# Squared deviation from the row mean: eight tiles of one row per partition in place of four tiles of two rows

## The chip, the cores and the metric

One core of a Trainium2 chip. The metric is the device time of one execution in microseconds (us), median of several. The kernel before takes 84.68 us (three runs, 84.6 to 84.7). All runs quoted are of the fast state (granted clock 1.000 in each profile), and correct.

## The reference

```python
batch, dim = 1024, 4096                      # x is float32, axis = -1
mean = np.mean(x, axis=axis, keepdims=True)
return ((x - mean) ** 2).astype(np.float32)
```

16.78 MB are read and 16.78 MB written. Everything fits into SBUF at once, so each tile has its own buffer.

## The kernel before

```python
Q = 2
ntiles = B // (P * Q)                                   # 4 tiles
x_t = x.rearrange("(n p q) d -> n p (q d)", p=P, q=Q)   # 32 KiB contiguous per partition
out_t = out.rearrange("(n p q) d -> n p (q d)", p=P, q=Q)
# ... pools with one buffer per tile
for i in range(ntiles):
    x_tile = pool.tile([P, Q * D], mybir.dt.float32)
    nc.sync.dma_start(out=x_tile, in_=x_t[i])           # all loads, on SP's queue
    x_tiles.append(x_tile)
for i in range(ntiles):
    # ... views and small tiles
    nc.vector.reduce_sum(out=neg_sum, in_=x_tile, axis=mybir.AxisListType.X, negate=True)
    nc.vector.tensor_scalar_mul(out=neg_mean, in0=neg_sum, scalar1=inv_d)
    for q in range(Q):
        nc.scalar.activation(out=x_tile[:, q, :], in_=x_tile[:, q, :],
                             func=mybir.ActivationFunctionType.Square,
                             bias=neg_mean[:, q:q + 1], scale=1.0)
    nc.scalar.dma_start(out=out_t[i], in_=x_tiles[i])   # store, on ScalarE's queue
```

Of the kernel before, what the change touches and what calls it, by code (L numbers as in the profile page):

```python
# [2 lines left out]

os.environ.setdefault("NEURON_RT_ULTRASERVER_MODE", "4")

# [4 lines left out]


@with_exitstack
def kernel(
    ctx: ExitStack,
    tc: tile.TileContext,
    x: bass.AP,
    axis: bass.AP,
    out: bass.AP,
):  # L20
    nc = tc.nc

    B, D = x.shape
    P = nc.NUM_PARTITIONS
    Q = 2
    assert B % (P * Q) == 0
    ntiles = B // (P * Q)

    inv_d = 1.0 / float(D)

    x_t = x.rearrange("(n p q) d -> n p (q d)", p=P, q=Q)
    out_t = out.rearrange("(n p q) d -> n p (q d)", p=P, q=Q)

    pool = ctx.enter_context(tc.tile_pool(name="io", bufs=ntiles))
    stats = ctx.enter_context(tc.tile_pool(name="stats", bufs=ntiles))

    x_tiles = []
    for i in range(ntiles):
        x_tile = pool.tile([P, Q * D], mybir.dt.float32)
        nc.sync.dma_start(out=x_tile, in_=x_t[i])  # L40
        x_tiles.append(x_tile)

    for i in range(ntiles):
        x_tile = x_tiles[i].rearrange("p (q d) -> p q d", q=Q)
        neg_sum = stats.tile([P, Q], mybir.dt.float32)
        neg_mean = stats.tile([P, Q], mybir.dt.float32)
        nc.vector.reduce_sum(  # L47
            out=neg_sum,
            in_=x_tile,
            axis=mybir.AxisListType.X,  # L50
            negate=True,
        )
        nc.vector.tensor_scalar_mul(out=neg_mean, in0=neg_sum, scalar1=inv_d)  # L53

        for q in range(Q):
            nc.scalar.activation(  # L56
                out=x_tile[:, q, :],
                in_=x_tile[:, q, :],
                func=mybir.ActivationFunctionType.Square,
                bias=neg_mean[:, q:q + 1],  # L60
                scale=1.0,
            )
        nc.scalar.dma_start(out=out_t[i], in_=x_tiles[i])


# [1 line left out]
_INS = ['x', 'axis']  # L67
_OUTS = [((1024, 4096), 'float32')]
#: Inputs that are plain numbers.
_NUMBERS = {'axis': -1}  # L70


# [26 lines left out]
```

## Time and profile before

| | before |
|---|---|
| time, span | 84.68 us, 82.9 us |
| VectorE, ScalarE busy | 43%, 37% |
| load queue + store queue, share of 16 DMA engines | 48.6% + 47.0% |
| first DMA packet to end of last one | 1.75 to 81.72 us |

Read it from the bottom: the transfers fill the DMA engines from 2 us to the end, and the compute engines wait for them. The lines of the page, the windows and the timeline stand in the prediction below.

The trace has a record of every DMA packet, with start, duration and queue, but without the number of the DMA engine. Since each of the 16 engines takes one packet after another, the records can be strung into 16 chains: each packet goes to the engine whose last packet ended closest to its start. In the kernel before this gives 16 chains of 64 packets each. Neighbouring chains can be confused by a few nanoseconds (in other runs some come out one packet long or short); pauses that all but one engine make cannot. At a hole, "the slowest engine" means the chain that runs dry last.

### The profile page before, as it was taken

The numbers are of one execution on the slowest core, as the hardware profiler recorded it, in microseconds if no ns is written. First come the engines' busy times: TensorE is split into PE (matmuls) and PEld (weight loads), VectorE is DVE, ScalarE is ACT, GpSimd is POOL, SyncE is SP. The second block draws the span as 40 slices with busy tenths as digits, with TensorE's granted clock in tenths as the row PEclk, the third lists the DMA queues.
The fourth block names the chain that finished last, engine by engine and source line by source line (L and its number), as shares of the span: only waits on it lengthen the run. The fifth ranks groups of instructions, "written<-read, shape, count | busy, mean of one in ns | idle before, by whom it ended". The sixth has DMA issues, their size and how long they took to land.

```text
span 82.9 us, 75 instructions
## 1 busy us (share of the span) xinstructions
DVE 35.4 (43%) x8; ACT 30.5 (37%) x9; POOL 0.2 (0%) x4
## 2 busy tenths in 40 slices
DVE  0000007999599995999900000799950000000000
ACT  0000006000399917998099950000049990000000
POOL 0000000000000000000000000000000000000000
DMA  7779997997999899997997999899796996995990
GB/s 190 300 332 443 506 427 332 506 490 316 459 506 411 348 506 285 443 474 316 490 490 332 443 490 427 348 506 474 332 443 285 506 490 269 506 506 253 506 506 0
DMA packets 1153, 33.55 MB, mean 405 GB/s; under 512 B 129, under 2 KB 129, under 8 KB 129
## 3 DMA queue, kind: packets, MB, share of 16 engines
q1 hardware_dynamic: 576, 16.78, 48.6%
q10 hardware_dynamic: 576, 16.78, 47.0%
q14 instruction: 1, 0.00, 0.0%
HBM read 16.78 MB, written 16.78 MB: 405 GB/s over the span
## 4 chain that ended last, share of the span: by engine, by line
DMA 37%; DVE 21%; another core or an unknown queue 13%; ACT 5%; issue 4%; SPq 1%
DMA x_tile<-in_x_dram 37%; DVE neg_sum L47 21%; ACT x_tile L56 5%; SPq L40 1%; DVE neg_mean L53 0%
## 5 line engine op out<-in xcount | busy, mean ns | idle before, releaser
L47 DVE TENSOR_REDUCE neg_sum<-x_tile 128x2 f32<-128x8192 f32 x4 | 34.7, 8686 | 25.6 <-DMA x_tile<-in_x_dram 25.6
L56 ACT ACTIVATE x_tile<-x_tile,neg_mean 128x4096 f32<-128x4096 f32 x8 | 29.2, 3700 | 24.9 <-DVE neg_mean L53 24.9
L56 ACT ACT_TABLE_LOAD x1 | 1.3, 1283 | 13.1 <-DMA x_tile<-in_x_dram 13.1
L53 DVE TENSOR_SCALAR neg_mean<-neg_sum 128x2 f32<-128x2 f32 x4 | 0.7, 170 | 0.1
L80 POOL MEMSET const-bfloat16-1.0<- 128x1 bf16 x1 | 0.1, 102 | 0.0
L80 POOL MEMSET const-uint8-127<- 128x1 uint8 x1 | 0.1, 102 | 0.0
L80 POOL MEMSET const-float32-1.0<- 128x1 f32 x1 | 0.1, 99 | 0.0
L80 POOL MEMSET const-float32-0.0<- 128x1 f32 x1 | 0.1, 98 | 0.2 <-issue 0.2
## 6 DMA issues: line engine op xcount, KB each, us to landing
x_tile<-in_x_dram SPq DMA_DIRECT2D x4, 4096.0 KB, 26.2
out_dram<-x_tile ACTq DMA_DIRECT2D x4, 4096.0 KB, 17.4
```

The source lines that it names most:

```text
L40: nc.sync.dma_start(out=x_tile, in_=x_t[i])
L47: nc.vector.reduce_sum(out=neg_sum, in_=x_tile, axis=mybir.AxisListType.X, negate=True,)
L53: nc.vector.tensor_scalar_mul(out=neg_mean, in0=neg_sum, scalar1=inv_d)
L56: nc.scalar.activation(out=x_tile[:, q, :], in_=x_tile[:, q, :], func=mybir.ActivationFunctionType.Square, bias=neg_mean[:, q:q + 1], scal ...
L80: nc = _bacc.Bacc("TRN2", target_bir_lowering=False, num_devices=1)
```

## The change

Its intent: finer tiles, so that the first reduction and the first store begin earlier and loads, arithmetic and stores overlap more. The loads stay on SP's queue and the stores on ScalarE's, as they were.

```diff
-    Q = 2
-    ntiles = B // (P * Q)
+    ntiles = B // P
-    x_t = x.rearrange("(n p q) d -> n p (q d)", p=P, q=Q)
-    out_t = out.rearrange("(n p q) d -> n p (q d)", p=P, q=Q)
+    x_t = x.rearrange("(n p) d -> n p d", p=P)
+    out_t = out.rearrange("(n p) d -> n p d", p=P)
@@ second loop, cut
-        for q in range(Q):
-            nc.scalar.activation(out=x_tile[:, q, :], in_=x_tile[:, q, :], ...
+        nc.scalar.activation(out=tiles[i], in_=tiles[i], ...
```

More of the change, by code (lines that the diff above doesn't have):

```diff
@@ L10 @@
 from concourse._compat import with_exitstack
+F32 = mybir.dt.float32
 @with_exitstack
@@ L24 @@
     P = nc.NUM_PARTITIONS
-    Q = 2
-    assert B % (P * Q) == 0
-    ntiles = B // (P * Q)
+    assert B % P == 0
+    ntiles = B // P
     inv_d = 1.0 / float(D)
-    x_t = x.rearrange("(n p q) d -> n p (q d)", p=P, q=Q)
-    out_t = out.rearrange("(n p q) d -> n p (q d)", p=P, q=Q)
-    pool = ctx.enter_context(tc.tile_pool(name="io", bufs=ntiles))
-    stats = ctx.enter_context(tc.tile_pool(name="stats", bufs=ntiles))
-    x_tiles = []
+    x_t = x.rearrange("(n p) d -> n p d", p=P)
+    out_t = out.rearrange("(n p) d -> n p d", p=P)
+    io = ctx.enter_context(tc.tile_pool(name="io", bufs=ntiles))
+    stats = ctx.enter_context(tc.tile_pool(name="stats", bufs=2 * ntiles))
+    tiles = []
     for i in range(ntiles):
-        x_tile = pool.tile([P, Q * D], mybir.dt.float32)
+        x_tile = io.tile([P, D], F32)
         nc.sync.dma_start(out=x_tile, in_=x_t[i])
-        x_tiles.append(x_tile)
+        tiles.append(x_tile)
     for i in range(ntiles):
-        x_tile = x_tiles[i].rearrange("p (q d) -> p q d", q=Q)
-        neg_sum = stats.tile([P, Q], mybir.dt.float32)
-        neg_mean = stats.tile([P, Q], mybir.dt.float32)
+        neg_sum = stats.tile([P, 1], F32)
+        neg_mean = stats.tile([P, 1], F32)
         nc.vector.reduce_sum(
-            out=neg_sum,
-            in_=x_tile,
-            axis=mybir.AxisListType.X,
-            negate=True,
+            out=neg_sum, in_=tiles[i], axis=mybir.AxisListType.X, negate=True
         )
         nc.vector.tensor_scalar_mul(out=neg_mean, in0=neg_sum, scalar1=inv_d)
-        for q in range(Q):
-            nc.scalar.activation(
-                out=x_tile[:, q, :],
-                in_=x_tile[:, q, :],
-                func=mybir.ActivationFunctionType.Square,
-                bias=neg_mean[:, q:q + 1],
-                scale=1.0,
-            )
-        nc.scalar.dma_start(out=out_t[i], in_=x_tiles[i])
+        nc.scalar.activation(
+            out=tiles[i],
+            in_=tiles[i],
+            func=mybir.ActivationFunctionType.Square,
+            bias=neg_mean,
+            scale=1.0,
+        )
+        nc.scalar.dma_start(out=out_t[i], in_=tiles[i])
 _INS = ['x', 'axis']
```

## The prediction

> **What bounds the kernel now.** I read four views in this order: the page (busy shares, DMA queues), the table of windows, the timeline, and the time from issue to landing of the two transfers. The page first:
>
> ```profile
> span 82.9 us, 75 instructions
> DVE 35.4 (43%) x8; ACT 30.5 (37%) x9; POOL 0.2 (0%) x4
> q1 hardware_dynamic: 576, 16.78, 48.6%
> q10 hardware_dynamic: 576, 16.78, 47.0%
> HBM read 16.78 MB, written 16.78 MB: 405 GB/s over the span
> ```
>
> No compute engine is half busy, while the two DMA queues (q1 the loads, q10 the stores) together take 48.6 + 47.0 = 95.6% of the 16 DMA engines' span. 576 packets per queue are four transfers of 128 rows (512 packets of 32 KiB) and 64 small completion writes. So the kernel is bound by bytes moved, and the question is only in which stages the DMA engines are not full. The windows answer it (the last two columns are DMA share and GB/s):
>
> ```profile
> 2.20:31.00 28.80, 17.10 (x3) 8.59 (x3) 0.00 (x0) 1.00 0.98 422
> 33.40:51.60 18.20, 7.92 (x2) 12.89 (x4) 0.00 (x0) 1.00 1.00 430
> 61.20:62.05 0.85, 0.00 (x0) 0.85 (x1) 0.00 (x0) 1.00 0.10 39
> 62.05:81.40 19.35, 0.00 (x0) 6.45 (x2) 0.00 (x0) 1.00 1.01 432
> 1.75:81.70 79.95, 35.43 (x8) 30.51 (x9) 0.00 (x0) 1.00 0.99 419
> ```
>
> Loads alone run at 422 GB/s, loads and stores mixed at 430, stores alone at 432: reading and writing together cost nothing. There is one hole, 61.20 to 62.05 us. The timeline shows who made it:
>
> ```profile
> 13.04 8.69 DVE L47 TENSOR_REDUCE neg_sum<-x_tile 128x2 f32<-128x8192 f32 x1 [13.04 <-DMA x_tile<-in_x_dram]
> ...
> 29.30 0.38 ACTq L63 DMA_DIRECT2D out_dram<-x_tile  x1
> ...
> 41.40 0.34 ACTq L63 DMA_DIRECT2D out_dram<-x_tile  x1
> 45.00 3.69 ACT L56 ACTIVATE x_tile<-x_tile,neg_mean 128x4096 f32<-128x4096 f32 x1
> 52.27 8.69 DVE L47 TENSOR_REDUCE neg_sum<-x_tile 128x2 f32<-128x8192 f32 x1 [10.92 <-DMA x_tile<-in_x_dram]
> 60.99 0.17 DVE L53 TENSOR_SCALAR neg_mean<-neg_sum 128x2 f32<-128x2 f32 x1
> 61.20 3.71 ACT L56 ACTIVATE x_tile<-x_tile,neg_mean 128x4096 f32<-128x4096 f32 x1 [12.50 <-DVE neg_mean L53]
> 61.20 0.34 ACTq L63 DMA_DIRECT2D out_dram<-x_tile  x1
> ```
>
> Tile 2 was squared at 45.00 + 3.69 = 48.7 us, but its store was issued at 61.20, beside the first activation of tile 3: in ScalarE's program that store stands behind an activation that has to wait for the last load and its 8.69 us reduction. By 61.2 the store queue had run dry.
>
> The trace's packet records give the rest of the budget. One 32 KiB packet takes 1.213 us on its engine, each engine has 64 of them: 64 x 1.213 = 77.6. The first packet starts at 1.75. The first packet of each engine is slow (0.70 us over the rest, averaged over the 16 engines), and when the first store joins the loads, the loads lose another 0.67. With 0.1 of small change and the hole of 0.85: 1.75 + 0.70 + 77.6 + 0.67 + 0.1 + 0.85 = 81.7, which is where the packets end. The last landing is 0.4 later, the end of the program 0.8 after that (82.9), and the time is 84.68, 1.8 over the span.
>
> **What the Trainium skill says.** (1) "DMA: Bandwidth & Descriptors", section Where 436 GB/s comes from: a fabric ceiling of 435.2 GB/s for the 16 ports. The trace agrees: 16 x 32,768 B / 1.213 us = 432 GB/s, so the steady stages have less than 1% to give. (2) Same page, Issuing engines are not separate DMA queues: issues from different engines end on the same 16 DMA engines and interleave. The trace agrees, and "loads on SP's queue, stores on ScalarE's" is moreover already so in the kernel before. (3) Same page, Queues, rings and completion order: each DMA engine goes round-robin over its queues by packet. The trace agrees: the last load, with 9.7 us of packets per engine, began at 31.5 and landed only at 52.2, as it should at half the rate. (4) "VectorE: DVE Perf Modes", the tier table: tensor_reduce has the 1x rate alone, at 0.96 GHz; 8192 elements would take 8.53 us, the trace has 8.69. So halving the row count halves the instruction.
>
> **The change, part by part.** Bytes, buffers in all, engines and queues stay. What changes is grain.
>
> Packets: 128 of 16 KiB per engine instead of 64 of 32 KiB. In the records an 8 KiB packet[...] takes 0.307 us at best and a 32 KiB one 1.211, so the slope is 0.904 us per 24,576 B and the fixed part 0.307 - 0.301 = some 6 ns. A 16 KiB packet is then 0.608 us (an estimate), and 128 x 0.608 = 77.9: **+0.3 us**, all of it on the path.
>
> VectorE: 8 reductions of 8.69 / 2 = 4.35 (say 4.4) and 8 scalings of 0.17, beside the transfers. ScalarE: the same 8 activations of 3.70. SP: 8 issues of some 0.45 us instead of 4, done by 5 us, while the first tile alone feeds the engines until some 7; nothing.
>
> First tile: lands after 8 packets of 0.608 instead of 1.213, so at 13.0 - 4.8 = 8.2. Reduction to 12.8, activation to 16.5, store issued then instead of at 29.3. In the kernel before it took 4.1 us from that issue (29.30) to the first store packet (33.41), behind packets already under way; I take 2.5 to 4.1 now, so stores start at 19.0 to 20.6. This gains **nothing** by itself: the engines are full with loads at that time, so stores only take turns with loads earlier.
>
> The end: I walk it with stores from 19.0. Loaded by then: (19.0 - 2.9) / 4.87 = 3.3 tiles (4.87 us is a tile alone, 9.73 at half rate). The other 4.7 loads take 4.7 x 9.73 = 45.7, so the last load is in at 64.7; 4.7 tiles are stored by then, and 3.3 remain, 16.1 us, to 80.8. Is the store queue ever dry? The compiled order on ScalarE is Act0, St0, Act1, Act2, St1, St2, Act3, Act4, St3, St4, Act5, Act6, St5, St6, Act7, St7, so the odd stores are still held behind the next activation. St3 goes with the start of Act4: tile 4 lands at 35.5, plus 4.5 is 40.0; needed at 48.2. St5 goes with Act6: 55.0 + 4.5 = 59.5; needed at 67.4 at the latest, some 66 at the earliest. St7: 64.7 + 0.5 (landing) + 4.5 + 3.7 = 73.4, plus 0.85 from issue to first packet = 74.3; St6 ends at 80.8 - 4.87 = 75.9. Margin 1.6 us, and more if the stores start later. So the hole goes: **-0.85 us**.
>
> Sum: 81.7 + 0.3 - 0.85 = 81.1 for the last packet, span 82.3, time 84.1. I add 0.2 for unevenness between the 16 engines, which twice as many landings may expose: **84.3 us**, 0.4% faster.
>
> **The rivals.** (a) A new hole at the end: if one engine lags by over 1.6 us at the last load, St7 comes late. For it: one load packet took 2.2 us when the stores joined, and the last load's 16 landings spread over 2.2 us. Against: the others spread over about 1 us or less. It would cost 0.5 to 1.5: 84.8 to 85.8. (b) The longer mixed stage (19 to 65 instead of 33 to 52) or the smaller packets run slower. For it: the 0.67 us lost when the stores joined. Against: 430 GB/s in the mixed window. If each 16 KiB packet lost 20 ns more, 128 x 0.02 = 2.6 us: 86.9, slower by over 2%. (c) A real gain from the earlier start, as the change intends: overlap of load, compute and store. Against: the DMA engines are full from 2 us on. Even with the hole, the joining loss and the slow first packets all gone, it is 84.68 - 0.85 - 0.67 - 0.70 = 82.5; 2% faster is 83.0, so nearly all three would have to go, and two of them are untouched.
>
> **Range and chances.** The low end, 83.6, is the sum with half of the joining loss gone; the high end, 85.4, is rival (a) in its middle. Faster by over 2% 0.02, slower 0.05 (rival b, or a hole of 2 us), within 2% 0.93.
>
> **What would show it.** Right: two queues of 1152 packets at 47 to 49% each; first reduction near 8.2 us, first store issue near 16.5; last load landing near 65; DMA at 430 GB/s through 20 to 80 with no window of 1 us or more empty; reductions near 4.4 us. Wrong: a mixed stage under 420 GB/s (rival b), or DMA idle before the last store (rival a). If reductions or activations end the chain with DMA idle beside them, my picture of a transfer-bound kernel fails.

## The result, and the profile after

| | before | after | foretold |
|---|---|---|---|
| time, first comparison | 84.65 us (4 runs) | 84.69 us (4 runs, 84.46 to 84.75) | 84.3 |
| ratio, first comparison | | 1.0002, 95% interval 0.9983 to 1.0020 | 0.9955 |
| ratio, second comparison | | 0.9983, 0.9962 to 1.0004 | 0.9955 |
| last DMA packet ends | 81.72 us | 81.81 us | 81.1 |

A ratio is the mean time of one kernel's fast runs over that of the other's in the same rounds, so it is not quite the ratio of the medians. All outputs are right. The time did not move: the range and "within 2%" held, the small gain (0.4%) did not come.

The page after, the same lines:

```profile
span 83.0 us, 96 instructions
DVE 36.6 (44%) x16; ACT 30.9 (37%) x9; POOL 0.2 (0%) x4
q1 hardware_dynamic: 1152, 16.78, 49.0%
q10 hardware_dynamic: 1152, 16.78, 47.2%
HBM read 16.78 MB, written 16.78 MB: 404 GB/s over the span
```

Twice the packets for the same bytes at the same share. The timeline after (start, duration, what):

```profile
8.58 4.42 DVE L46 TENSOR_REDUCE neg_sum<-x_tile 128x1 f32<-128x4096 f32 x1 [8.58 <-DMA x_tile<-in_x_dram]
...
16.96 0.38 ACTq L57 DMA_DIRECT2D out_dram<-x_tile  x1
...
60.10 4.07 ACTq L57 DMA_DIRECT2D out_dram<-x_tile  x2
65.17 4.42 DVE L46 TENSOR_REDUCE neg_sum<-x_tile 128x1 f32<-128x4096 f32 x1 [5.11 <-DMA x_tile<-in_x_dram]
...
73.55 0.34 ACTq L57 DMA_DIRECT2D out_dram<-x_tile  x1
```

The first store goes at 16.96 instead of 29.30, as intended; the last reduction begins later than before (65.17, not 52.27), because the loads now share the engines with stores for longer. The windows after (last two columns: DMA share, GB/s):

```profile
17.00:22.00 5.00, 4.68 (x3) 3.71 (x1) 0.00 (x0) 1.00 0.98 364
22.00:64.00 42.00, 19.21 (x10) 18.54 (x5) 0.00 (x0) 1.00 1.00 430
61.20:62.05 0.85, 0.00 (x0) 0.85 (x1) 0.00 (x0) 1.00 0.99 424
```

The hole of the kernel before (0.85 us at share 0.10) is filled: 0.99. And there is no other one. Yet the last packet ends no earlier. So what was the hole worth?

The packet chains answer. This is how each engine of the kernel **before** went through the hole (worked out from the packet records, ns; one number per engine):

```
pause at 62 us, 16 engines: 0 170 402 497 574 584 616 623 657 705 741 756 797 824 866 898   mean 607
```

The engine with pause 0 is the one that ends the kernel: it was still at its store packets until 62.36 us, while the others had run dry from 61.27 on and had begun again between 62.05 and 62.17. Then the ends of the last packet:

| us | first engine | mean | last engine |
|---|---|---|---|
| before | 81.53 | 81.59 | 81.72 |
| after | 81.12 | 81.34 | 81.81 |
| after, second profile | 81.00 | 81.22 | 81.63 |

The change did make the mean engine earlier, by 0.25 to 0.37 us. The last one, which the kernel waits for, stayed within 0.1 us of where it was.

### The profile page after: what moved, and what is told of

Same layout as the page of the kernel before. It is cut to its first block, busy times and chain, and to the rows that moved or that the text cites. A ratio compares the mean times of both kernels' runs of the same rounds, so it can differ in the third digit from the quotient of the medians.

```text
span 83.0 us, 96 instructions
## 1 busy us (share of the span) xinstructions
DVE 36.6 (44%) x16; ACT 30.9 (37%) x9; POOL 0.2 (0%) x4
## 3 DMA queue, kind: packets, MB, share of 16 engines
q1 hardware_dynamic: 1152, 16.78, 49.0%
q10 hardware_dynamic: 1152, 16.78, 47.2%
## 4 chain that ended last, share of the span: by engine, by line
DMA 77%; DVE 6%; ACT 4%; SPq 1%; issue 0%
DMA x_tile<-in_x_dram 77%; DVE neg_sum L46 5%; ACT x_tile L50 4%; SPq L40 1%; DVE neg_mean L49 0%
## 5 line engine op out<-in xcount | busy, mean ns | idle before, releaser
L46 DVE TENSOR_REDUCE neg_sum<-x_tile 128x1 f32<-128x4096 f32 x8 | 35.4, 4420 | 32.9 <-DMA x_tile<-in_x_dram 32.9
L50 ACT ACTIVATE x_tile<-x_tile,neg_mean 128x4096 f32<-128x4096 f32 x8 | 29.7, 3708 | 33.9 <-DVE neg_mean L49 33.9
L49 DVE TENSOR_SCALAR neg_mean<-neg_sum 128x1 f32<-128x1 f32 x8 | 1.2, 154 | 0.3
```

Of the source, the lines that this page charges most:

```text
L46: nc.vector.reduce_sum(out=neg_sum, in_=tiles[i], axis=mybir.AxisListType.X, negate=True)
L50: nc.scalar.activation(out=tiles[i], in_=tiles[i], func=mybir.ActivationFunctionType.Square, bias=neg_mean, scale=1.0,)
```

## The experiments

Two theories. **A**: the end is set by the slowest of the 16 DMA engines; in the hole only the faster ones waited for it, so filling it gives them time that nobody needs. **B**: the hole cost the kernel 0.6 (mean pause) to 0.85 us as predicted, and something in the finer grain costs as much. Each ratio is to the kernel before on the same chip, in five rounds.

### The hole alone: queues exchanged, two-row tiles

```diff
-        nc.sync.dma_start(out=x_tile, in_=x_t[i])
+        nc.scalar.dma_start(out=x_tile, in_=x_t[i])
-        nc.scalar.dma_start(out=out_t[i], in_=x_tiles[i])
+        nc.sync.dma_start(out=out_t[i], in_=x_tiles[i])
```

> The kernel before with the queues exchanged: loads issued by ScalarE, stores by SP, so that no store stands behind an activation and the third store goes at about 49 us, not 61.2. The hole at 61.2 closes. Theory A (the end is set by the slowest of the 16 DMA engines, which never paused in that hole; only the 15 faster ones did): 84.5 to 84.75 us, no gain. Theory B (the hole cost all engines 0.6 to 0.85 us, and the finer packets of the change ate the gain): 83.8 to 84.1 us.

Measured: 84.58 us (six runs, 84.03 to 84.85), ratio 0.9975 (0.9949 to 1.0000). The third store goes at 48.71, and the window of the hole is full (the share counts packets at their start, so it can pass 1 in a short window):

```profile
48.71 0.33 SPq L63 DMA_DIRECT2D out_dram<-x_tile  x1
```

```profile
61.20:62.05 0.85, 0.04 (x1) 0.77 (x1) 0.00 (x0) 1.00 1.35 578
62.05:81.40 19.35, 0.00 (x0) 6.53 (x2) 0.00 (x0) 1.00 0.95 410
```

No engine pauses by more than 0.05 us any more. The first engine ends at 80.66, the mean at 80.99, the last at 81.91: the mean engine gained the whole 0.60 us, the last gained nothing (81.72 before). (The profiled run of this kernel was the slowest of its six, 84.85 us.) The second line shows it from the other side: 410 GB/s at the end, where the kernel before had 432, because engines that are done idle beside the late ones. That is A. It isn't all of it: the ratio says 0.2 us with an interval from 0 to 0.4, and one of six runs came at 84.03, as B would have it. A guess, not shown: without a hole the time depends on how unequal the engines happen to be in that execution. These six runs scatter over 0.82 us, the kernel before over 0.37 in the same rounds; but the changed kernel, which has no hole either, scatters over 0.29 us and, in the second comparison, 0.12.

### The control: queues exchanged, one-row tiles

The same edit in the changed kernel.

> The changed kernel with the queues exchanged in the same way: no store is held behind an activation. There was no hole in the changed kernel, so both theories say the same: 84.5 to 84.8 us. A time under 84.2 would say that the holding back of the odd stores cost something that neither theory has.

Measured: 84.64 us, ratio 0.9988 (0.9972 to 1.0005). As foretold: the exchange of queues and the end of the holding back of every second store, taken together, change nothing.

### The grain alone: two-row tiles, 16 KiB packets

```diff
-    x_t = x.rearrange("(n p q) d -> n p (q d)", p=P, q=Q)
-    out_t = out.rearrange("(n p q) d -> n p (q d)", p=P, q=Q)
+    x_t = x.rearrange("(n q p) d -> n p q d", p=P, q=Q)
+    out_t = out.rearrange("(n q p) d -> n p q d", p=P, q=Q)
```

> The kernel before with its two-row tiles, engines and order, but the two rows of a partition lie 128 rows apart, so every packet is 16 KiB. Only the grain of the transfers changes. Theory A (some 6 ns more per packet, 64 packets more on each DMA engine, +0.4 us, less what a shorter first and joining packet gives back): 84.7 to 85.1 us. Theory B (the grain costs as much as the hole was worth, 0.6 to 0.85): 85.25 to 85.5 us.

Measured: 84.64 us, ratio 0.9989 (0.9975 to 1.0003): below both ranges, so A missed here too. The packets are not free: on one engine they follow each other every 607 ns instead of two in 1210, and in the changed kernel every 607.8, so 128 x 0.6078 - 64 x 1.2097 = 0.38 us per engine. But this kernel still has the hole, and the records show that it swallowed the cost: the mean pause is 0.25 us instead of 0.61, and the last engine ends at 81.67. Whatever an engine loses ahead of the hole, it loses out of its own waiting time. For the same reason the time of this run alone can't exclude a grain cost of B's size: a cost up to the mean pause, 0.61 us, could have been swallowed too. The spacing does, with 0.38 us instead of 0.6 to 0.85, and so does the next run. (In this trace the engine that ends last, at 81.67, did pause, by 0.41 us; the one that didn't pause ends at 81.58. All 16 ends lie within 0.15 us.)

### The grain, four times finer

SBUF tiles of the changed kernel padded every 4 KiB (`x_wide = io.tile([P, 4, D // 4 + 8], F32)`, used through `x_wide[:, :, : D // 4]`), so that each packet is 4 KiB; the reduction runs over both inner axes.

> The changed kernel with SBUF tiles padded every 4 KiB, so that packets are 4 KiB: 512 per DMA engine instead of 128. Theory A, 5.8 ns fixed per packet: 384 more make +2.2 us, 86.7 to 87.2 us. Theory B, 64 more packets cost 0.6 to 0.85 us, so 9 to 13 ns each: 384 more make +3.6 to +5.1 us, 88.3 to 89.8 us.

Measured: 86.47 us, ratio 1.0201 (1.0184 to 1.0217). Against the exchanged one-row kernel (84.64), +1.8 us; A's range began 0.2 us higher, B's 1.8. On one engine packets follow each other every 155.5 ns: 512 x 0.1555 - 128 x 0.6078 = +1.8 us. From 4 and 16 KiB the fixed part is 4.7 ns per packet, from 16 and 32 KiB 5.8. There is no hole here to hide it. So the prediction's term for the grain (+0.3) was right, with some luck: its 6 ns came from 8 KiB packets of another queue, which the profile calls instruction packets.

### A hole on purpose, short and long

A copy in place between the last activation and the last store of the changed kernel, over 2400 or 4096 columns:

```diff
+        if i == ntiles - 1:
+            nc.scalar.activation(out=tiles[i][:, :2400], in_=tiles[i][:, :2400],
+                                 func=mybir.ActivationFunctionType.Copy)
         nc.scalar.dma_start(out=out_t[i], in_=tiles[i])
```

> The changed kernel with a copy of 2400 columns in place between the last activation and the last store: the last store is issued at some 75.9 instead of 73.55, its first packets at some 76.8. In the trace of the changed kernel the 16 DMA engines end the store before between 76.3 and 76.95, so most engines pause, the slowest does not. Theory A (the slowest engine sets the end): no cost, within 0.15 us of the changed kernel. Theory B (mean idle of the engines counts): +0.3 us.

> The same with 4096 columns: the last store is issued at some 77.35, its first packets at some 78.2, 1.25 us after the slowest engine has run dry and 1.7 after the mean one. Theory A: +1.1 to +1.4 us over the changed kernel. Theory B: +1.6 to +1.8 us.

And beside them, as their base:

> The changed kernel unchanged, for a closer interval and as the base of the two delays of the same call. All theories: 84.5 to 84.8 us, within 0.3% of the kernel before.

Measured: base 84.56 us (0.9983); short 84.65 (0.9992, 0.9967 to 1.0017); long 85.92 (1.0140, 1.0115 to 1.0165). The timeline of the long one:

```profile
73.53 3.62 ACT L58 ACTIVATE x_tile<-x_tile 128x4096 f32<-128x4096 f32 x1
77.18 0.34 ACTq L63 DMA_DIRECT2D out_dram<-x_tile  x1
```

and its window at the hole, in which no packet starts at all:

```profile
76.60:78.00 1.40, 0.00 (x0) 0.55 (x1) 0.00 (x0) 1.00 0.00 0
```

In the long one the engines paused 1.11 us (the slowest) to 1.98, on average 1.71; the time rose by 85.92 - 84.56 = 1.36. That lies in A's range and below B's. In the short one 13 of 16 engines paused, up to 0.49 us and 0.20 on average, the last to end did not; the time rose by 0.09. This agrees with A, but the intervals are as wide as the 0.2 to 0.3 us that B asks for, so the short one alone would decide nothing.

### Where the engines grow unequal

In the records of before, most of it comes at two places: the first packet of each engine (up to 1.2 us over the rest) and the moment when the first store's packets join the loads (0.67 us per engine on average before, 0.66 after, 0.4 to 1.5 on single engines). The slowest engine of before started at 2.27, lost 0.55 in its first packet and some 1.4 at the joining; with 64 x 1.210 = 77.4 that makes 81.7, its end, with no pause in it.

Is the joining loss one of the store queue's first use?

> The changed kernel with the load of the second tile alone on ScalarE's queue, which the stores use later. Two questions: does a start from two queues fill the engines sooner (a gain of up to 0.3 us), and is the loss when the first store joins (0.66 us per engine) one of a queue's first use (then it vanishes, and with it part of the spread between the engines: 84.0 to 84.3 us) or of two queues beginning to share an engine (then it stays: 84.4 to 84.8)? I expect the second.

Measured: 84.48 us, ratio 0.9970 (0.9949 to 0.9992), within the range of the answer that I expected. Load packets are long by 0.83 us per engine around 28 to 30 us, when the stores join. First use is not it. The edit did one more thing: tile 0 now shares the engines with tile 1, so the first reduction begins at 12.90 us and the first store is issued at 26.13, not near 17. As for the first question, the engines' first packets start at 1.87 us on average, against 1.90 in the unchanged kernel of the same call: no gain to speak of. The 0.1 us against that kernel's time (84.56) is within the noise.

### When the stores begin

```diff
+        if i == 0:
+            zero = stats.tile([P, 1], F32)
+            nc.gpsimd.tensor_scalar_mul(out=zero, in0=tiles[6][:, 0:1], scalar1=0.0)
+        if i < 6:   # the store cannot go before load 6 has landed
+            nc.gpsimd.tensor_tensor(out=tiles[i][:, 0:1], in0=tiles[i][:, 0:1], in1=zero,
+                                    op=mybir.AluOpType.add)
         nc.scalar.dma_start(out=out_t[i], in_=tiles[i])
```

> The changed kernel with all stores held until the load of tile 6 has landed, some 37.5 us instead of 17.0 (GpSimd adds 0 times a column of tile 6 to a column of tiles 0 to 5; the result stays right). The DMA engines still have the last load to do when the stores begin, so they never run dry. Theory A (bytes on always full engines set the time; when stores begin is worth nothing): 84.4 to 85.0 us. The intent of the change (storing earlier shortens the run): 20 us less overlap should show as several us.

Measured: 84.36 us (84.15 to 84.38), ratio **0.9953** (0.9940 to 0.9966). The first store is issued at 38.44 us:

```profile
38.44 5.16 ACTq L66 DMA_DIRECT2D out_dram<-x_tile  x6
```

The time is 0.04 us under A's range. Stores that begin 21 us later make it not slower but slightly faster than the kernel before, and probably than the changed one, which was compared with it only in other calls (1.0002 and 0.9983). The intent of the change, storing earlier, is worth nothing here. The hold also let SP issue all eight loads by 4.85 us, where the changed kernel issued the last at 18.34; that isn't the gain, since the control with exchanged queues issued its eight by 4.95 us and ran at 0.9988. The five microseconds in which stores take over, to set beside 17 to 22 us of the changed kernel above (0.98 and 364 GB/s):

```profile
38.50:43.50 5.00, 4.01 (x3) 2.83 (x1) 0.67 (x5) 1.00 0.99 419
43.50:80.00 36.50, 4.51 (x2) 7.42 (x2) 0.00 (x0) 1.00 1.01 432
```

The same share, but 419 GB/s: **busy is not moving**. In the changed kernel the load packets stretched while the stores joined and the share stayed near 1; only the rate shows it. Here the last load's packets are long by 0.07 us per engine instead of 0.66. The first store's packets began at 41.65, just as the loads ran out. All engines end earlier: first 80.55, mean 80.84, last 81.31.

Held until the last load, on the other hand, all 16 engines run dry together:

> The same, held until the last load has landed (some 42.5 us). Now all 16 engines run dry, the slowest too, from its last load packet (some 42.2) over the landing, two small GpSimd instructions and the issue to the first store packet, some 1.5 to 2 us; loads and stores never share an engine, so the joining loss (0.66) and its part of the spread go. Theory A: 85.2 to 86.2 us.

Measured: 86.62 us, ratio 1.0227 (1.0213 to 1.0241), above my range.

```profile
41.60:44.10 2.50, 2.19 (x3) 1.68 (x1) 1.11 (x7) 1.00 0.00 0
```

The pauses were 1.93 us on the engine with the shortest and 2.72 on the longest; I had counted 1.5 to 2. The rest of the miss: after such a common restart packets followed each other every 613.7 ns instead of 607.8 (64 x 5.9 = 0.4 us). The kernel before shows the same after its hole, 1217 ns against 1209.7 ahead of it. Why is open.

Held until load 4 only:

> As the hold until the load of tile 6 (which ran at 0.9953 of the kernel before, with no joining loss in its packets), but held only until the load of tile 4 has landed, some 27.5 us; the first stores are issued at some 28.3 and their packets should join at some 31.5, with about two loads still queued. If the loss of 0.5 to 0.8 us per engine comes whenever stores join a load queue that still has work, it is back: loads' packets long by that much around 31, 84.5 to 84.8 us (0.998 to 1.001 of the kernel before). If it came only of an early or a first use, it stays away: 0.994 to 0.997, 84.2 to 84.45 us.

Measured: 84.51 us, ratio 0.9971 (0.9951 to 0.9991): the time is at the foot of the first answer's range, the ratio between the two. The packets show the loss back in part: 0.42 us per engine around 31 to 33 us, when two loads were still queued. So the loss has to do with stores joining a queue that still has loads, and is smaller when fewer are left; what in the engine makes it is open.

A last attempt, three two-row tiles and then two of one row, with the same hold:

> An attempt to beat both: three tiles of two rows (32 KiB packets), then two of one row; stores held until the fourth load has landed (some 37.5 us), so that they follow the loads without a gap and hardly share the engines with them. Against the hold until load 6: 80 packets per engine instead of 128, 48 x 5.8 ns = 0.28 us less at best; the grain experiment showed about nothing of it in the time. 84.0 to 84.4 us, 0.992 to 0.996 of the kernel before.

Measured: 84.37 us, ratio 0.9950 (0.9934 to 0.9966). Inside the range, and no better than the simple hold: the packets saved (48 x 5.8 ns = 0.28 us) were probably given back where the stores took over, as the last load's packets there were long by 0.79 us per engine on average. Half a per cent is what I found to be had; whether more can be had is open.

## Why the prediction was wrong, point by point

- **What bounds it, and the flow of events**: right. Queues of 1152 packets at 49.0 and 47.2%; first reduction at 8.58 (8.2 foretold), first store issue 16.96 (16.5), its first packets 20.93 (19.0 to 20.6), last reduction 65.17 (65.2), last store issue 73.55 (73.4), no window empty.
- **Grain, +0.3**: right: 0.38 by the spacing of packets.
- **The hole, "-0.85 us"**: this is the step that failed. The hole did go; its worth was mis-sized. I took a window in which the share of 16 engines fell to 0.10 as time that every engine lost. The records show pauses of 0 to 0.9 us, 0.61 on average, and 0 on the engine that ended last and that the kernel waits for. With the hole alone removed, the time fell by 0.2 us (0 to 0.4), and the last packet not at all in the profiled run.
- **The budget that seemed to confirm it**: its sum met the measured end (81.7), but it mixes averages over 16 engines (0.70, 0.67) with the pause of the faster ones (0.85). No engine has that sum. A sum that fits is no evidence when its terms belong to different queues.
- **"+0.2 for unevenness"**: the right subject in the wrong place. The gap from the mean to the last engine's end was 0.13 us before and 0.47 after (0.41 in the second profile), because the hole had evened the engines out and its absence didn't. It is the hole and not the number of landings: two-row tiles without a hole have a gap of 0.92 us, 16 KiB packets with a hole 0.09.

The balance, for the mean engine: -0.61 (pause gone), -0.12 (16 packets x 7.3 ns, the slow spacing after the restart, gone), +0.38 (grain), +0.15 (first packets and the pauses between them: 0.85 per engine instead of 0.70), -0.04 (the joining with its pauses: 0.70 instead of 0.74) = -0.24, measured -0.25. Then +0.34 for the last engine behind the mean: +0.09, as measured (81.72 to 81.81).
- **Rival (c)**, that earlier overlap would pay: rightly dismissed; holding the stores back by 21 us cost nothing. **Rivals (a), (b)**: no new hole; the mixed stage runs at 430 GB/s, and the loss at the joining is of the same size as before.
- **Two slips that cost nothing**: "SP done by 5 us" was wrong; in the changed kernel SP issued loads 7 and 8 at 13.44 and 18.34 us, after waiting for earlier loads (14.2 us in two waits). More than three loads were still queued each time (by the packets already started), so the engines didn't notice. And 83.6, the low end of the range, is 84.3 less the whole joining loss (0.67), not half of it.

## What to carry to other kernels

Here, with all DMA engines full, finer tiles and earlier stores only moved work about inside a fixed total. In such a case first ask for the rate (bytes by GB/s), then for holes, and for each hole whether the engine that runs dry last was in it. A hole is worth about the pause of that engine, not the mean pause of the 16: 0.2 us (0 to 0.4) for pauses of 0 and 0.61 in the kernel before, 1.36 for 1.11 and 1.71 in the long delay. A change that removes a hole can free 15 engines and not the kernel. And watch the rate beside the busy share: engines can be busy at 364 GB/s where they do 430 elsewhere.

## What the Trainium skill lacked or had wrong

- "DMA: Bandwidth & Descriptors", Latency and other measured facts, gives some 600 ns to the first byte from SP's and ScalarE's queues. It doesn't say where that time begins. Here it took 0.85 us from the start of the issuing instruction to the first packet (0.5 from its end) with idle engines (61.20 to 62.05 before; 77.18 to 78.02 in the long delay), and 3.2 to 4.1 us with engines full of loads (29.30 to 33.41 before, 16.96 to 20.93 after, 38.44 to 41.65 in the hold).
- That a bulk transfer goes at the pace of its slowest engine stands on that page only as an aside (iDMA fabric). Nothing says how far the 16 drift apart within one kernel: 0.7 us in the changed kernel, 1.25 with the queues exchanged; nor that a hole which the last engine to run dry isn't in is all but free (0.09 us in the short delay).
- No page that I found has the loss when stores join a queue of loads: 0.4 to 0.9 us per engine, at a busy share of 0.98 (17 to 22 us of the changed kernel).
- No page that I found gives the fixed cost of a packet on these two queues as a time (the DMA page counts it in cycles): here 4.7 to 5.8 ns.
